# State-space scan moved from VectorE to GpSimd, with low parts moved the other way and masked bias tiles, in a hybrid S5 and attention layer

## The chip, the core and the metric

The kernel runs on one core of a Trainium2 chip. A core has TensorE (PE in the profile; its weight loads are PEld), VectorE (DVE), ScalarE (ACT), GpSimd (POOL) and SyncE (SP), which here issues the transfers. The metric is the device time of one execution, in microseconds, as a median of runs. For the kernel before, that is 2432.99 us (3 runs, 2431.76 to 2434.61).

## The reference, cut to what matters

One layer on x of 2048 tokens by 1024, in float32. Half of the mixing is a diagonal state-space layer, half is chunked attention; then an output projection and a SwiGLU.

```python
proj = rmsnorm(x, norm_mix_g) @ w_in                 # u (512), q, k, v (512 each)
# state-space layer: 32 groups of 16 channels, 64 complex states in each group
states = associative_scan(lam_bar * left + bu)       # bu = b_bar @ u, over 2048 tokens
y_ssm = glu(gelu((c @ states).real + d * u))
# attention: 8 heads of 64; a chunk of 64 frames sees itself and the 8 chunks before
scores = q @ k.T / 8 + bias[h, clip(rel, -128, 128)] # -1e30 outside the band
y_att = softmax(scores) @ v
x = x + concat(rmsnorm(y_ssm), rmsnorm(y_att)) @ w_out
x = x + (silu(h2 @ w_gate) * (h2 @ w_up)) @ w_down   # h2 = rmsnorm(x); then a final rmsnorm
```

## The kernel before, in words

Nearly every product of matrices is made of three matmuls: an operand is split into a high part (a rounded copy, by ACT) and a low part (raw less high, a subtraction by DVE or POOL), and the products high by high, high by low and low by high are summed (`mm3`, `split`, L151).

The phases, with their times in the profiled execution:

1. The input of the state-space layer is projected (`u_phase`, about the first 150 us). Beside it DVE works out the powers of the decay and the tables of the layer (`ssm_prologue`). The tables pass through tensors in HBM.
2. Attention and the state-space layer run interleaved (`att_phase`, about 150 to 830 us). Attention is 128 steps: 4 blocks of 512 tokens, 4 pairs of heads, 2 heads, 4 groups of 128 queries. Of each step come the scores (PE; then DVE adds the bias and takes the minimum, L736; then ACT takes the exponential, L739), two steps later the transposes (PE L77; ACT copies the high part, L754; DVE makes the low part, L755), and after a head's four groups the product with v.
3. Between these, "units" are advanced by a fixed number of yields per step: the projections of q and k (`qk_unit`) and v (`v_unit`) for each block, the normalised input of the block (`hT_unit`: DVE product L638, ACT high part L639, low part L640), and the eight units of the state-space layer (`ssm_unit`), 15 steps each.
4. The mixing, gate, up and down products follow (`mix_phase` and later, to the end).

One unit of the state-space layer takes four groups of 16 channels. It loads its input U and three tables, waits 8 yields, multiplies U with a table, and ACT copies the result into X (L511; 128 partitions, 2 parts, 2 pairs, 256 positions). Then comes the scan on the engine `eng`: seven steps over each eighth position (L525 to L528, four instructions on 128 elements per partition), seven over the ends of the eights in groups (16 elements), three over the groups (4 elements), and the carries back (L536 and L537, 42 and 434 elements). That is 84 instructions. Then four transfers copy the states into XG in another layout (L557), nine yields pass, and PE multiplies U and XG with two tables (`pj<-U,Tm` and `pj<-XG,Vm`).

PE's instructions are kept in the written order (`keep_in_program_order`), so PE stands still at an instruction whose data are late. The other engines and SP take their instructions in an order that the framework's scheduler fixes when the program is built; within an engine the order is then strict, too.

Other places that the change touches: `load_w` (weights of attention are loaded raw, split, and in the first block stored to HBM at L613 for the later blocks, which load them at L615); the bias tile `nb` of each head (loaded at L715 at the head's first step; two memsets on POOL at L716 and L717 put 1e30 into the two corners of 64 by 64 outside the band); and the memset of XG's first column (L554). `k.ssm_eng` and `k.wlo_eng` name the engines of the scan and of the weights' low parts.

Of the kernel before, what the change touches and what calls it, by code (L numbers as in the profile page):

```python
# [13 lines left out]
ALU = mybir.AluOpType  # L14
AX = mybir.AxisListType

P = 128
# [3 lines left out]
NG, CH, NS = 32, 16, 64  # L21
NPR = NG // 2
L = 8
NC = SEQ // L
GB, GP = 4, 2
# [66 lines left out]
def f32(ap):  # L92
    return ap.bitcast(F32)
# [297 lines left out]
def u_phase(k, ident, S):  # L391

    tc, nc, io = k.tc, k.nc, k.io
    with ExitStack() as cx:
        p2 = cx.enter_context(tc.tile_pool(name="u2", side="right", bufs=2))
        p1 = cx.enter_context(tc.tile_pool(name="u1", side="right", bufs=1))
        p3 = cx.enter_context(tc.tile_pool(name="u3", side="right", bufs=4))
        psum = cx.enter_context(tc.tile_pool(name="ups", bufs=6, space=bass.MemoryType.PSUM, reuse_waits="tile"))
        psum2 = cx.enter_context(tc.tile_pool(name="ups2", bufs=2, space=bass.MemoryType.PSUM, reuse_waits="tile"))
        k.pro_psum = psum2  # L400
        wh, wl = k.t(p1, "wuh", [P, KT, DS], F32R), k.t(p1, "wul", [P, KT, DS], F32R)
        rsn = S["rsn"][:].rearrange("p (c j) -> p j c", j=L)
        te = k.te
        X, ST = {}, {}

        def prep(b, each=None):
            acc = k.t(p2, "acc", [P, 512])
            X[b] = []
            for q in range(KT):
                if b == 0:  # L410
                    raw = k.t(p2, "raw", [P, DS])
                    nc.sync.dma_start(raw[:], io["w_u"][q * P : (q + 1) * P, :])
                    nc.scalar.activation(wh[:, q, :], raw[:], AF.Copy, scale=k.gm[:, q : q + 1])
                    nc.vector.scalar_tensor_tensor(wl[:, q, :], raw[:], k.gm[:, q : q + 1], f32(wh[:, q, :]),
                                                   op0=ALU.mult, op1=ALU.subtract)
# [24 lines left out]
        def spread_(b):  # L440
            ps = k.t(psum2, "pp", [P, 512])
            spread(k, te, ps, ST[b], 0)
            nc.scalar.copy(rsn[:, 2 * b : 2 * b + 2, :], ps[:].rearrange("p (j c) -> p j c", j=2))

        def evac(b, f, ps):
            us = k.t(p3, "us", [P, 2, NC], bufs=2)
            nc.vector.tensor_tensor(us[:], ps[:].rearrange("p (j c) -> p j c", j=2), rsn[:, 2 * b : 2 * b + 2, :], op=ALU.mult)
            nc.sync.dma_start(S["u"][f * P : (f + 1) * P, 2 * b : 2 * b + 2, :], us[:])

        def group(b, f):  # L450
            ps = k.t(psum, "ps", [P, 512])
            for q in range(KT):
                mm(b, f, ps, q)
            return ps

        def finish(b, pss):
            with tc.high_priority():
                spread_(b)
                for f in range(4):
                    evac(b, f, pss[f])  # L460

        pss = [k.t(psum, "ps", [P, 512]) for _ in range(4)]

        def first(q):
            for f in range(4):
                mm(0, f, pss[f], q)

        pro = ssm_prologue(k, ident, S)
        prep(0, first)
        next(pro)  # L470
        sums(0)
        held = pss
        for b in range(1, 4):
            prep(b)
            next(pro)
            now = [group(b, 0)]
            finish(b - 1, held)
            now += [group(b, 1), group(b, 2)]
            sums(b)
            held = now + [group(b, 3)]  # L480
        next(pro)
        finish(3, held)
    return pro


def ssm_unit(k, p, psum, S, b, eng):
# [62 lines left out]
    yield from carry(Xe[:, :, :, 1:, :7], Xe[:, :, :, :3, 7], 8, 3)  # L549
    yield from carry(Xk[:, :, :, 1:, :7], Xk[:, :, :, : NC // 8 - 1, 7], 0, NC // 8 - 1)  # L550

    XG = k.t(p, "XG", [P, GB, NC])
    XGv = XG[:].rearrange("p (q g) c -> p q g c", g=2)
    nc.gpsimd.memset(XG[:, :, 0:1], 0.0)  # L554
    for g2 in range(2):
        for c in range(2):
            nc.sync.dma_start(XGv[c * NS : (c + 1) * NS, :, g2, 1:], X[g2 * NS : (g2 + 1) * NS, c, :, : NC - 1])  # L557
    for _ in range(YX):
        yield
    Y = k.t(p, "X", [P, GB, NC])  # L560
# [10 lines left out]
        yield  # L571


SSM_N = YL + GP + 7 + 7 + 3 + 4 + YX + GP


class Unit:
# [21 lines left out]
def att_phase(k, ident, S, pro):  # L599
    tc, nc, io = k.tc, k.nc, k.io  # L600
    with ExitStack() as cx:
        aw = tc.alloc_tile_pool(name="aw", reuse_waits="tile", bufs=1, side="right")
        pfs = cx.enter_context(tc.tile_pool(name="apf", bufs=2, space=bass.MemoryType.PSUM, reuse_waits="tile"))
        hT, vts, qk = {}, {}, {}

        def load_w(sb, n):

            w = k.t(aw, "w", [P, 2, 1024], F32R, bufs=WB)
            if sb == 0:
                raw = k.t(aw, "raw", [P, 1024], bufs=2)  # L610
                nc.sync.dma_start(raw[:], io["w_qk"][n] if n < 8 else io["w_v"][n - 8])
                split(k, w[:, 0], w[:, 1], raw[:], k.wlo_eng)
                nc.sync.dma_start(S["ws"][n], f32(w[:]))  # L613
            else:
                nc.sync.dma_start(f32(w[:]), S["ws"][n])  # L615
            return w[:, 0], w[:, 1]

        def hT_unit(sb, q0=0, q1=KT):
            hi, lo = hT.setdefault(sb, ([], []))
# [12 lines left out]
            for q in range(q0, q1):  # L632
                yield
                load(q + ahead)
                xt = xts[q]
                for v, n in zip(hT[sb], ("hi", "lo")):
                    v.append(k.t(aw, f"{n}{q}x" if q < DB and sb % 2 else f"{n}{q}", [P, SB], F32R))
                nc.vector.scalar_tensor_tensor(xt[:], xt[:], k.gm[:, q : q + 1], S["rsn"][:, ts], op0=ALU.mult, op1=ALU.mult)  # L638
                nc.scalar.copy(hi[q][:], xt[:])  # L639
                (nc.gpsimd if sb or q % 2 else nc.vector).tensor_tensor(lo[q][:], xt[:], f32(hi[q][:]), op=ALU.subtract)  # L640
            yield

        def qk_unit(sb, pr):
# [11 lines left out]
            for c in range(2):  # L655
                ps = k.t(pfs, "pf", [P, 512])
                wh, wl = ws[c]
                for q in range(KT):
                    cs = slice(q * P, (q + 1) * P)
                    mm3(k.ta, ps[:], wh[:, cs], wl[:, cs], hi[q][:], lo[q][:], q == 0, q == KT - 1)  # L660
                    if q < KT - 1:
                        yield
                for hh in range(2):
# [17 lines left out]
        def v_unit(sb, fh):  # L681
# [5 lines left out]
            for i in range(4):  # L687
                ps = k.t(pfs, "pf", [P, 256])
                ic = slice(i * P, (i + 1) * P)
                for q in range(KT):  # L690
# [4 lines left out]
                    k.ta.matmul(ps[:], lo[q][:, ic], wh, start=False, stop=q == KT - 1)  # L695
                    if q % 2 and q < KT - 1:
                        yield
                vt = vts[4 * sb + i, fh]
                pv3 = ps[:].rearrange("p (h d) -> p h d", h=4)
                nc.scalar.copy(vt[:, :, :HD], pv3)  # L700
# [5 lines left out]
        class Head:  # L706
            pass

        def scores(st):
            sb, pr, hh, qp = st  # L710
            h = 2 * pr + hh
            if qp == 0:
                hd = st_head[sb, h] = Head()
                hd.nb = k.t(aa, "nb", [P, 640], bufs=2)
                nc.sync.dma_start(hd.nb[:], bass.AP(S["nb"].tensor, S["nb"].offset + h * 768 + 1, [[1, P], [1, 640]]))  # L715
                nc.gpsimd.memset(hd.nb[0:64, 0:64], 1e30)  # L716
                nc.gpsimd.memset(hd.nb[64:128, 576:640], 1e30)  # L717
                hd.s = {}
                hd.p = None
            hd = st_head[sb, h]  # L720
            q2h, q2l, k2 = qk[sb, pr][hh]
            k0 = max(qp, 4) if sb == 0 else qp
            nk = (qp + 5 - k0) * P
# [762 lines left out]
def block_kernel(tc, io, phases="pusamf"):  # L1486
    nc = tc.nc
    k = K(tc, io)
    k.ssm_eng, k.wlo_eng = nc.vector, nc.gpsimd
    with ExitStack() as cx:  # L1490
        dram = cx.enter_context(tc.tile_pool(name="dram", bufs=1, space=bass.MemoryType.DRAM))
        cp = cx.enter_context(tc.tile_pool(name="const", bufs=1))
# [2 lines left out]
        def pp():  # L1495
# [2 lines left out]
        S = {  # L1498
            "u": k.t(dram, "u", [DS, L, NC]), "y": k.t(dram, "y", [DS, L, NC]),
            "ya": k.t(dram, "ya_s", [NSB, DS, SB]), "x1": k.t(dram, "x1", [D, SEQ]),  # L1500
            "k": k.t(dram, "ks", [2, H, P, SB]), "nb": k.t(dram, "nbs", [H, 768]),
            "bst": k.t(dram, "bsts", [4, P, 8 * P]), "v": k.t(dram, "vs", [NPR, 2, 2, NS, 9 * CH]),
            "hc": k.t(dram, "hc", [2, 7, P, 4, 512]), "h": k.t(dram, "hs", [4, P, HALF]), "ws": k.t(dram, "wss", [12, P, 2, 1024]),
            "hq": k.t(dram, "hq", [2, F2, 7, P, 512]), "wc": k.t(dram, "wc", [F2, 7, P, 512]), "wt": k.t(dram, "wt", [4, P, HALF]),
# [81 lines left out]
```

## Time and profile before

| what | value |
|---|---|
| median of 3 runs | 2432.99 us (2431.76 to 2434.61) |
| profiled execution | 2425.27 us |
| its span, first to last instruction | 2423.5 us |
| mean granted TensorE clock | 0.964 |
| DMA | 425.75 MB |
| 200 to 800 us: PE busy | 523.21 us |
| 200 to 800 us: DVE busy | 456.27 us |
| 200 to 800 us: ACT busy | 300.44 us |
| 200 to 800 us: POOL busy | 58.36 us |

A row of a view by stages gives a stretch of the span, its length, and for each engine the busy time and the number of instructions, then the granted clock, the share of the DMA engines and the rate. A row of a timeline gives start, duration, engine, line, operation, `out<-in` with shapes, and in brackets the idle time of the engine before it and what ended that. A row of waits says who waited for whom: total, times, longest.

### The profile page before, as it was taken

Reading aid. Unit: us, or ns where it says so; the run is one execution under the profiler, and the core shown is the slowest. Engines: PE = TensorE matmul, PEld = TensorE weight load, DVE = VectorE, ACT = ScalarE, POOL = GpSimd, SP = SyncE. Lnnn points to the kernel's source line nnn. Section 1 sums busy time; section 2 is a strip of 40 time slices with the busy share of each in tenths; the row PEclk is TensorE's granted clock in tenths of the full one; section 3 lists DMA queues with packets and bytes.
Section 4 is the critical chain, followed back from the end, with each engine's and each line's share of the span. In section 5 each row is a group of like instructions: output and inputs, shape, how many; then the busy total and the mean of one; then the engine's idle time right before and its main releaser. Section 6 shows DMA issues by size and latency. Waiting matters only on the chain.

```text
span 2423.5 us, 30933 instructions
## 1 busy us (share of the span) xinstructions
PE 2224.6 (92%) x10744; PEld 1862.5 (77%) x10744; DVE 1665.3 (69%) x2943; ACT 1000.3 (41%) x1671; POOL 909.0 (38%) x613
## 2 busy tenths in 40 slices
PE   6876878899998799999999999899999989999996
PEld 5655767788787678877888888688888868888886
DVE  8965688777878675656676666867655456569676
ACT  4233544455544754234333334433333343345322
POOL 4321210010100043257555555755555554445542
PEclk8887999999999999999999999999999989999998
DMA  5655676566554353564455455645433277555551
GB/s 159 174 194 203 216 206 199 174 192 191 169 176 123 121 170 122 183 229 149 135 183 177 158 187 206 237 170 202 154 122 95 71 295 253 190 200 200 182 191 70
DMA packets 223132, 425.75 MB, mean 176 GB/s; under 512 B 30384, under 2 KB 70832, under 8 KB 215872
## 3 DMA queue, kind: packets, MB, share of 16 engines
q1 hardware_dynamic: 222976, 423.79, 53.6%
q8 instruction: 84, 1.38, 0.2%
q14 instruction: 72, 0.59, 0.1%
HBM read 283.97 MB, written 129.26 MB: 171 GB/s over the span
## 4 chain that ended last, share of the span: by engine, by line
PE 56%; DVE 2%; DMA 2%; POOL 1%; issue 1%; ACT 1%; SPq 0%; DVEq 0%; POOLq 0%; ACTq 0%
PE X L74 18%; PE ps L74 18%; PE Y L74 9%; PE big L74 6%; PE W L74 5%; DMA lo<-hc 1%; DVE lo L151 1%; POOL c L151 0%; POOL lo L151 0%; POOL sa L1005 0%; DMA hd<-wc 0%; POOL sa L1004 0%; DVE acc L1451 0%; DVE S L1253 0%; DVE g L1318 0%
## 5 line engine op out<-in xcount | busy, mean ns | idle before, releaser
L74 PE MATMUL X<-hi,c 128*128 128x512 f32 x1408 | 451.2, 391 | 7.9 <-POOL c L151 3.2
L74 PE MATMUL ps<-hd,hd 128*128 128x512 f32 (+1 forms) x1968 | 434.7, 383 | 8.0 <-DVE hd L151 4.6
L74 PEld LDWEIGHTS ps<-hd,hd 128*128 128x128 f32 x1968 | 361.3, 191 | 80.1 <-DVE hd L151 4.9
L151 POOL TENSOR_TENSOR c<-S,c 128x512 fp32r<-128x512 f32 x176 | 251.8, 1432 | 243.8 <-ACT c L150 239.8
L74 PEld LDWEIGHTS X<-hi,c 128*128 128x128 f32 x1408 | 265.1, 188 | 65.5 <-ACT u L1271 4.0
L74 PE MATMUL X<-lo,c 128*128 128x512 f32 x704 | 274.9, 390 | 0.0
L151 POOL TENSOR_TENSOR hd<-hd 128x1536 fp32r<-128x1536 f32 (+1 forms) x53 | 190.3, 3596 | 208.7 <-ACT hd L150 185.5
L150 ACT CAST hd<-hd 128x1536 fp32r<-128x1536 f32 (+1 forms) x106 | 147.4, 1392 | 227.1 <-DMA hd<-hq 155.3
L151 POOL TENSOR_TENSOR c<-raw,c 128x512 fp32r<-128x512 f32 x132 | 189.6, 1436 | 130.6 <-ACT c L150 105.5
L74 PE MATMUL Y<-hi,c 128*128 128x512 f32 x704 | 227.2, 393 | 11.3 <-DVE u L1275 11.3
L1399 DVE TENSOR_TENSOR acc<-acc,ps 128x512 f32<-128x512 f32 x196 | 129.2, 682 | 87.0 <-PE ps L74 84.4
L74 PE MATMUL pf<-hi,w 128*128 128x512 f32 x416 | 157.7, 428 | 10.5 <-ACT hi L639 10.5
L74 PEld LDWEIGHTS Y<-hi,c 128*128 128x128 f32 x704 | 133.5, 190 | 41.0 <-DVE u L1275 13.0
L74 PE MATMUL big<-m,woh 128*128 128x512 f32 x512 | 163.7, 402 | 0.2 <-DVE yr L941 0.2
L150 ACT CAST c<-S 128x512 fp32r<-128x512 f32 x176 | 109.3, 621 | 114.6 <-PE Y L74 57.8
L74 PEld LDWEIGHTS X<-lo,c 128*128 128x128 f32 x704 | 132.7, 188 | 27.3
L716 POOL MEMSET nb<- 64x64 f32 x32 | 4.6, 144 | 387.9 <-DMA nb<-nbs 246.0
L1271 ACT COPY u<-X 128x512 f32<-128x512 f32 x132 | 76.9, 584 | 176.4 <-PE X L74 176.4
L739 ACT ACTIVATE s<-s,mn 128x640 f32<-128x640 f32 (+4 forms) x128 | 97.9, 765 | 121.4 <-DVE mn L736 102.9
L150 ACT CAST c<-raw 128x512 fp32r<-128x512 f32 x132 | 82.1, 622 | 149.7 <-PE Y L74 82.3
L736 DVE CUSTOM_DVE_ANT_0 s<-sc,nb 128x640 f32<-128x640 f32 (+4 forms) x128 | 94.1, 735 | 70.5 <-PE sc L74 56.6
L151 DVE TENSOR_TENSOR hd<-hd 128x1536 fp32r<-128x1536 f32 (+1 forms) x53 | 113.4, 2141 | 35.7 <-ACT hd L150 35.6
(370 smaller groups left out, 4812.2 us busy)
## 6 DMA issues: line engine op xcount, KB each, us to landing
w<-wss SPq DMA_DIRECT2D x36, 1024.0 KB, 5.5
hq<-g SPq DMA_DIRECT2D x140, 256.0 KB, 2.1
hd<-hq SPq DMA_DIRECT2D x42, 768.0 KB, 4.5
hd<-wc SPq DMA_DIRECT2D x42, 768.0 KB, 6.0
raw<-in_w_gate SPq DMA_DIRECT2D x44, 512.0 KB, 3.8
raw<-in_w_up SPq DMA_DIRECT2D x44, 512.0 KB, 4.2
wc<-px SPq DMA_DIRECT2D x66, 256.0 KB, 2.9
wss<-w SPq DMA_DIRECT2D x12, 1024.0 KB, 4.4
```

What stands on the lines that cost most here:

```text
L74: return self.tc.keep_in_program_order(self.tc.nc.tensor.matmul(*a, **b))
L150: nc.scalar.copy(hi, raw)
L151: (lo_eng or nc.gpsimd).tensor_tensor(lo, raw, f32(hi), op=ALU.subtract)
L716: nc.gpsimd.memset(hd.nb[0:64, 0:64], 1e30)
L736: nc.vector.tensor_tensor_reduce(s[:, :nk].rearrange("p (a b) -> p a b", a=nch), ps[:, :nch, :half], hd.nb[:, nk - 1 :: -1].rearrange("p ( ...
L739: nc.scalar.activation(s[:, :nk], s[:, :nk], AF.Exp, bias=mn[:], scale=-1.0, accum_out=sums[sb, pr][:, hh, qp : qp + 1])
L1271: nc.scalar.copy(u[:], ps[:])
L1399: V.tensor_tensor(a, a, ps[:], op=ALU.add)
```

## The change

- `k.ssm_eng` becomes GpSimd: the whole scan runs on POOL. The four transfers of its states (L557) are issued by the same engine, so they move from SP's queue to POOL's.
- XG is one tile for all units; its first column is set to zero once.
- `k.wlo_eng` becomes VectorE: the low parts of the 12 attention weight tiles move from POOL to DVE. So do the low parts of `hT_unit` in all blocks but the first (24 instructions).
- The bias tiles with their corners are written once to a new tensor `nbm` in HBM, in the first phase: one copy from HBM to HBM, and two copies of a constant tile into the corners. A head loads its finished tile, without a memset, and the load is issued two steps before the head begins.
- The stores of split weights (L613) are issued later: in `qk_unit` after the third of eight slices of the product, in `v_unit` after the first of four groups of rows.

```diff
@@ u_phase
+            if b == 2:
+                corner = k.t(p1, "corner", [64, H, 64])
+                nc.gpsimd.memset(corner[:], 1e30)
+                nc.sync.dma_start(S["nbm"][:], bass.AP(S["nb"].tensor, S["nb"].offset + 1, [[768, H], [1, P], [1, 640]]))
+                for m in range(2):
+                    nc.sync.dma_start(S["nbm"][:, m * 64 : m * 64 + 64, m * 576 : m * 576 + 64].rearrange("h p c -> p h c"), corner[:])
@@ ssm_unit
-    XG = k.t(p, "XG", [P, GB, NC])
+    if b == 0:
+        k.XG = k.t(p, "XG", [P, GB, NC])
+        nc.gpsimd.memset(k.XG[:, :, 0:1], 0.0)
+    XG = k.XG
-    nc.gpsimd.memset(XG[:, :, 0:1], 0.0)
...
-            nc.sync.dma_start(XGv[c * NS : (c + 1) * NS, :, g2, 1:], X[g2 * NS : (g2 + 1) * NS, c, :, : NC - 1])
+            eng.dma_start(XGv[c * NS : (c + 1) * NS, :, g2, 1:], X[g2 * NS : (g2 + 1) * NS, c, :, : NC - 1])
@@ att_phase
-                nc.sync.dma_start(S["ws"][n], f32(w[:]))
+                keep[n] = w
...
+        def keep_w(n):
+            if n in keep:
+                nc.sync.dma_start(S["ws"][n], f32(keep.pop(n)[:]))
...
-                (nc.gpsimd if sb or q % 2 else nc.vector).tensor_tensor(lo[q][:], xt[:], f32(hi[q][:]), op=ALU.subtract)
+                (nc.vector if sb or q % 2 == 0 else nc.gpsimd).tensor_tensor(lo[q][:], xt[:], f32(hi[q][:]), op=ALU.subtract)
...
+                    if q == 2:
+                        keep_w(4 * c + pr)
...
+                if i == 0:
+                    for r in range(2):
+                        keep_w(8 + 2 * r + fh)
...
+        def load_nb(h):
+            nb = k.t(aa, "nb", [P, 640], bufs=2)
+            nc.sync.dma_start(nb[:], S["nbm"][h])
+            return nb
...
-                hd.nb = k.t(aa, "nb", [P, 640], bufs=2)
-                nc.sync.dma_start(hd.nb[:], bass.AP(S["nb"].tensor, S["nb"].offset + h * 768 + 1, [[1, P], [1, 640]]))
-                nc.gpsimd.memset(hd.nb[0:64, 0:64], 1e30)
-                nc.gpsimd.memset(hd.nb[64:128, 576:640], 1e30)
+                hd.nb = nbs.pop(h) if nbs else load_nb(h)
...
+            if qp == 2 and (sb, h) < (NSB - 1, H - 1):
+                nbs[(h + 1) % H] = load_nb((h + 1) % H)
@@ block_kernel
-    k.ssm_eng, k.wlo_eng = nc.vector, nc.gpsimd
+    k.ssm_eng, k.wlo_eng = nc.gpsimd, nc.vector
...
-            "k": k.t(dram, "ks", [2, H, P, SB]), "nb": k.t(dram, "nbs", [H, 768]),
+            "k": k.t(dram, "ks", [2, H, P, SB]), "nbm": k.t(dram, "nbms", [H, P, 640]), "nb": k.t(dram, "nbs", [H, 768]),
```

More of the change, by code (lines that the diff above doesn't have):

```diff
@@ L571, in ssm_unit @@
         yield
-SSM_N = YL + GP + 7 + 7 + 3 + 4 + YX + GP
+SSM_N = YL + GP + 7 + 7 + 3 + 4  + YX + GP
 class Unit:
@@ L603, in att_phase @@
         pfs = cx.enter_context(tc.tile_pool(name="apf", bufs=2, space=bass.MemoryType.PSUM, reuse_waits="tile"))
-        hT, vts, qk = {}, {}, {}
+        hT, vts, qk, keep = {}, {}, {}, {}
         def load_w(sb, n):
@@ L707, in att_phase @@
             pass
+        nbs = {}
+        def load_nb(h):
+            nb = k.t(aa, "nb", [P, 640], bufs=2)
+            nc.sync.dma_start(nb[:], S["nbm"][h])
+            return nb
         def scores(st):
```

## The prediction

> **What bounds the kernel now.** I read the page first, then split the stretch in which the state-space layer's eight scans run (217 to 783 us) into the time inside a scan and the time between two scans, then the waits of PE, then single rows. The page says that PE is the busiest engine over the span, so time can be won only where PE stands still:
>
> ```profile
> PE 2224.6 (92%) x10744; PEld 1862.5 (77%) x10744; DVE 1665.3 (69%) x2943; ACT 1000.3 (41%) x1671; POOL 909.0 (38%) x613
> ```
>
> The stages from the first to the last DVE instruction of each scan, and those between, alternate here (columns: length, then busy time and count of PE, PEld, DVE, ACT, POOL, then granted clock and DMA):
>
> ```profile
> 217.60:255.50 37.90, 23.78 (x104) 19.29 (x104) 35.94 (x113) 15.52 (x36) 10.10 (x10) 0.77 0.55 192
> 255.50:297.70 42.20, 36.70 (x216) 32.23 (x217) 20.08 (x54) 21.28 (x58) 10.24 (x10) 0.92 0.72 230
> 297.70:342.50 44.80, 32.46 (x147) 25.45 (x146) 42.39 (x135) 19.17 (x51) 8.18 (x10) 0.92 0.69 209
> 342.50:374.80 32.30, 28.79 (x198) 26.51 (x196) 15.41 (x34) 17.01 (x42) 3.27 (x7) 1.00 0.74 193
> 374.80:417.80 43.00, 37.59 (x210) 31.67 (x208) 41.59 (x124) 20.27 (x39) 0.58 (x4) 1.00 0.64 201
> 417.80:446.50 28.70, 26.17 (x184) 24.73 (x183) 13.21 (x26) 15.48 (x35) 0.40 (x3) 1.00 0.53 129
> 446.50:491.70 45.20, 37.96 (x212) 32.43 (x211) 43.90 (x121) 21.89 (x41) 7.62 (x12) 0.96 0.63 201
> 491.70:524.90 33.20, 32.20 (x218) 29.86 (x217) 18.74 (x34) 19.62 (x41) 4.11 (x6) 1.00 0.73 203
> 524.90:567.00 42.10, 38.04 (x215) 33.22 (x214) 40.70 (x122) 18.99 (x36) 0.87 (x6) 0.96 0.60 192
> 567.00:596.10 29.10, 29.10 (x197) 27.28 (x196) 15.80 (x31) 17.54 (x37) 0.40 (x3) 1.00 0.68 200
> 596.10:638.30 42.20, 35.34 (x206) 30.10 (x206) 40.84 (x119) 19.93 (x38) 5.04 (x9) 0.97 0.53 165
> 638.30:671.40 33.10, 33.10 (x203) 29.99 (x203) 18.89 (x32) 18.95 (x38) 2.70 (x3) 0.98 0.64 171
> 671.40:708.00 36.60, 33.22 (x213) 29.23 (x212) 35.28 (x114) 15.86 (x32) 0.87 (x6) 1.00 0.56 185
> 708.00:744.40 36.40, 33.10 (x194) 29.30 (x193) 19.39 (x34) 20.00 (x40) 0.40 (x3) 1.00 0.56 157
> 744.40:782.50 38.10, 34.64 (x233) 31.63 (x232) 36.81 (x117) 16.72 (x33) 0.87 (x6) 1.00 0.40 120
> ```
>
> Inside a scan DVE is busy 95 to 97% of the time and PE idles 14.1, 12.3, 5.4, 7.2, 4.1, 6.9, 3.4 and 3.5 us, 56.9 in all. Between scans DVE is about half busy and PE idles 5.5, 3.5, 2.5, 1.0, 0, 0 and 3.3 us. So DVE is the limit inside the scans, PE outside, and POOL is nearly free in both. The waits of PE from 200 to 800 us name DVE too:
>
> ```profile
> PE pt L77 <- DVE ptl L755: 30.0, 30, 2.3
> PE sc L74 <- DVE mn L736: 16.4, 8, 10.5
> ```
>
> These two make 46.4 us (total, times, longest). Neither belongs to the scan: they are attention's own evictions, the low parts of the transposes and the minima of the scores, which queue on DVE behind the scan's instructions.
>
> **The scan leaves DVE: the gain.** I give each scan stretch the idle share of PE in the stretch behind it (0.130, 0.109, 0.088, 0.030, 0, 0, 0.091, and the last share again for the eighth). What is left is 4.9, 4.9, 3.8, 1.4, 0, 0, 3.3 and 3.4, together 21.7 us. The granted clock, 0.77 in the first scan and 0.92 in the second against 1.00 later, may rise with it; I count nothing for that. The gain is 56.9 - 21.7 = 35.2 us, by unit 9.2, 7.5, 1.6, 5.9, 4.1, 6.9, 0.1 and 0. At most all 56.9 could go. What is late next is PE itself in units 2 to 7, and in 0 and 1 the small steps of the first block of tokens.
>
> **The scan on POOL: how long.** POOL runs no such small instruction now, so its price comes from larger ones:
>
> ```profile
> 230.40 2.40 POOL L151 TENSOR_TENSOR w<-raw,w 128x1024 fp32r<-128x1024 f32 x1 [9.95 <-ACT w L150]
> 243.88 1.28 POOL L640 TENSOR_TENSOR lo0x<-xt,hi0x 128x512 fp32r<-128x512 f32 x1 [8.35 <-ACT hi0x L639]
> 897.31 1.28 POOL L1004 TENSOR_TENSOR sa<-sa,xt 128x512 f32<-128x512 f32 x1 [4.95 <-issue]
> 898.67 1.28 POOL L1005 TENSOR_TENSOR sa<-sa,xt 128x512 f32<-128x512 f32 x1
> ```
> ```profile
> L527 DVE TENSOR_TENSOR X<-X,st x136: 151/189/512, 218.1 to 770.8; 128x128 f32<-128x128 f32 x56, 128x16 f32<-128x16 f32 x56, 128x4 f32<-128x4 f32 x24
> ```
> ```profile
> L536 DVE TENSOR_TENSOR fx<-X,a x64: 153/596/2691, 239.1 to 781.2; 128x42 f32<-128x42 f32 x32, 128x434 f32<-128x434 f32 x32
> ```
>
> From 512 to 1024 elements POOL pays 1.12 us more: 2.19 ns an element and 0.16 us fixed. The dependent pair at 897 starts 1.36 us apart, 0.08 us over its duration. Four lines like L527 and two like L536, over eight units, give a unit 28 instructions of 128 elements (0.44 us), 28 of 16 (0.195), 12 of 4 (0.17), 8 of 42 (0.25) and 8 of 434 (1.11): 12.3 + 5.5 + 2.0 + 2.0 + 8.9 = 30.7 us, and with 84 gaps of 0.08, 37.4 us. Without the gaps it is 30.7; with half as much again for every one of the 7,888 elements (17.3 us) it is 46.0. I take 37.4, as both rows are of POOL and of the same operation.
>
> Then the four transfers of the states, now queued on POOL behind the scan, in two rows of the tile's view (the first with min, median and max in ns):
>
> ```profile
> L557 SPq DMA_DIRECT2D XG<-X x32: 590/611/1174, 266.0 to 783.2; - x32
> ```
> ```profile
> DMA to landing us min/median/max: 2.3/2.4/5.5
> ```
>
> At SP's price, 4 x 0.61 + 2.4 = 4.8 us; at the dearest, 4 x 1.17 + 5.5 = 10.2. No row has a transfer issued by POOL; I take 4.8. So scan and transfers take 42.2 us. The transfers wait on POOL for the last carry, and behind them stands only the next unit's scan, which needs its own X some 25 us later; SP, where the same waits stood in front of every load, is rid of them.
>
> The Trainium skill ("DMA: Bandwidth & Descriptors", Specifications) gives a first byte about 1 us after issue from GpSimd against 0.6 from Sync; by it 42.2 would be 42.6, and no run here shows it.
>
> **The room that PE leaves.** PE keeps its written order, so it stands still if the states are not there at its first matmul on XG:
>
> ```profile
> L74 PE MATMUL pj<-XG,Vm x64: 378/379/379, 275.1 to 795.2; 128*128 128x256 f32 x64
> ```
> ```profile
> L511 ACT COPY X<-pj x64: 363/367/370, 214.5 to 744.0; 64x256 f32<-64x256 f32 x64
> ```
>
> Eight copies and eight such matmuls belong to a unit. From the start of the scan, which follows the last copy, to the first such matmul there are 57.5 (275.1 - 217.6), 54.0, 52.8, 56.7, 52.3, 56.0, 52.6 and 48.0 us. Less the gains above: 48.3, 46.5, 51.2, 50.8, 48.2, 49.1, 52.5 and 48.0. All are above 42.2.
>
> **POOL and DVE against each other.** While POOL's split of 230.40 ran, a scan instruction of DVE on 16 elements took 2.25 us, where its sister L527, quoted above, has a median of 0.19 over all sizes:
>
> ```profile
> 230.58 2.25 DVE L525 TENSOR_TENSOR st<-X,a 128x16 f32<-128x16 f32 x1
> ```
>
> It ended with POOL's instruction. The Trainium skill ("SBUF — State Buffer", Who interferes with whom) explains it: a DVE instruction with two SBUF inputs and a GpSimd one that reads SBUF exclude each other for a whole instruction. The trace agrees. So each DVE instruction of this kind adds its length to POOL's scan. They are the products of L638, the low parts that move to DVE (24, of the blocks after the first) and the 12 weight splits:
>
> ```profile
> 217.60:262.60 45.00, 0.74 (x1) 0.77 0.60 215
> 297.70:342.70 45.00, 4.56 (x7) 0.92 0.69 209
> 446.50:491.50 45.00, 2.97 (x4) 0.96 0.63 201
> 596.10:641.10 45.00, 2.00 (x3) 0.96 0.56 170
> ```
> ```profile
> 217.60:262.60 45.00, 0.00 (x0) 10.38 (x4) 0.77 0.60 215
> ```
> ```profile
> 869.83 1.22 DVE L151 TENSOR_TENSOR wol<-xt,woh 128x1024 fp32r<-128x1024 f32 x1
> ```
> ```profile
> L640 DVE TENSOR_TENSOR lo<-xt,hi x1: 679/679/679, 169.3 to 169.3; 128x512 fp32r<-128x512 f32 x1
> ```
>
> The first fence counts L638 (DVE) in four scans, the second the splits (POOL). Unit 0 has 0.74 + 4 x 1.22 = 5.6 us, and 42.2 + 5.6 = 47.8 fits in 48.3. Unit 1 has 4.56 + 6 x 0.68 = 8.6: 50.8 against 46.5, a stall of 4.3 us. Unit 3 has 5.7 (47.9 against 50.8), unit 5 has 4.0 (46.2 against 49.1). The stall is 4.3 us in all.
>
> DVE's own added work, 24 x 0.68 + 12 x 1.22 = 31 us, lies in stretches that free over 20 us of DVE per unit: nothing on the path.
>
> **The mask, the stores and the start.** The tiles' two memsets per head go. DVE waited for POOL at these starts of heads:
>
> ```profile
> 273.85 0.29 DVE L736 CUSTOM_DVE_ANT_0 s<-sc,nb 128x128 f32<-128x128 f32 x1 [1.36 <-POOL nb L716]
> ```
> ```profile
> 655.97 0.82 DVE L736 CUSTOM_DVE_ANT_0 s<-sc,nb 128x640 f32<-128x640 f32 x1 [4.00 <-POOL XG L554]
> ```
>
> That is 5.4 us won, since the loads are also issued two steps ahead; if PE had been covered there it is 0. The XG memset becomes one. The stores of split weights leave SP's queue until the split is long done; SP, which queues every other load behind it, gains, and I price it at 0, as no wait of PE above names a weight load. The 12 splits at half POOL's time may win 2 us before 220 us. Against it, the masked tiles are built in HBM in the first phase: 2.6 MB plus corners that must wait on SP for the large copy, with the loads of xt behind them.
>
> ```profile
> DMA packets 223132, 425.75 MB, mean 176 GB/s; under 512 B 30384, under 2 KB 70832, under 8 KB 215872
> ```
>
> At this mean rate it takes 15 us, hidden as long as four tiles are ahead; from 0 to 8 us, I take 2.
>
> **Sum.** -35.2 + 4.3 - 5.4 - 2 + 2 = -36.3 us. The profiled execution took 2425.27 us (span 2423.5), so 2389 there; the median of the runs shown is 2432.99, 7.7 us above it, so 2397.
>
> **Rivals.**
> Scan too long (slower). If a small POOL instruction with several dimensions costs another 0.16 us, as much fixed cost again, a unit takes 42.2 + 13.4 = 55.6 us, and with the exclusion the stalls are 12.9, 17.7, 4.4, 10.5, 7.4, 10.5, 3.1 and 7.6, together 74 us: -35.2 - 5.4 + 74 = +33, 2466 us. It decides from about 51.3 us a unit, 9 us above my sum, or 0.11 us an instruction. For it: the trace has no small two-input instruction of POOL on several dimensions. Against it: the two sizes that the fit rests on leave only 0.16 us fixed, and the gap of 0.08 us is charged 84 times already. Chance 0.21.
>
> Steps over strided elements. The recurrences at L525 to L528 read every eighth float or further apart. If their 4,080 elements a unit cost half as much again, that is 4.5 us: 46.7, stalls 4.0, 8.8, 1.6 and 1.6 in units 0, 1, 3 and 5, and -35.2 - 5.4 + 16 = -24.6, 2408 us. Chance 0.16. The Trainium skill ("GPSIMD Engine Reference", Performance pitfalls for Q7 kernels) states about this surcharge for reads with steps above 8 bytes; no run here shows it.
>
> Nothing won. PE may follow ACT's copies rather than DVE, or the mask's building may cost what DVE yields: -4 to +4 us, 2429 to 2437. Against it: ACT is busy 41 to 48% in the scans and PE's waits name DVE. Chance 0.10.
>
> **How the numbers follow.** Forecast 0.53, with an own range of 2376 (all 56.9 us) to 2414 (10 us of stall more and no mask gain). A measurement here can tell 0.2%, 4.9 us. Faster: 0.53 + 0.16 and a little of the third, 0.71; same 0.07; slower 0.21 and 0.01, 0.22. The range goes from 2374 to 2446: below it little is left, above it about two thirds of the slow rival.
>
> **What the profile after would show.** Right: POOL near 40 us busy per unit, DVE near 55% in the scans, PE idle 3 to 13% there, the first XG matmul not waiting except in unit 1, and 200 to 800 us shorter by about 35. Wrong: PE waiting for XG in every unit (first or second rival), or the first phase longer by over 5 us, or PE still waiting for the softmax evictions with DVE idle.

## The result, and the profile after

The kernel after takes 2406.00 us (median of 4 runs, 2403.77 to 2413.88) beside 2432.38 us for the kernel before (4 runs, 2427.64 to 2434.61): a ratio of 0.990, 95% interval 0.9873 to 0.9927. It is faster by 26 us, where 36 was forecast. The profiled execution has a span of 2401.7 us against 2423.5, 21.8 us less.

The first part of the page of the kernel after shows where work has gone: DVE is 145 us less busy, POOL 228 us more.

```profile
PE 2214.6 (92%) x10744; PEld 1863.5 (78%) x10744; DVE 1520.6 (63%) x2307; ACT 999.0 (42%) x1671; POOL 1137.4 (47%) x1211
```

I cut both spans at three events that both kernels have: the last DVE product of the first phase (L447), ACT's last copy into the first unit's X, and PE's last matmul on XG. Stages of the kernel before (stretch, length, busy times and counts of PE, PEld, DVE, ACT, POOL, granted clock, DMA):

```profile
0.00:147.70 147.70, 112.09 (x480) 89.72 (x480) 132.02 (x360) 46.95 (x78) 44.25 (x36) 0.90 0.55 156
217.50:795.60 578.10, 503.47 (x2988) 442.42 (x2988) 448.77 (x1218) 288.77 (x610) 55.66 (x97) 0.96 0.62 185
795.60:2423.50 1627.90, 1557.80 (x7017) 1290.20 (x7015) 1059.76 (x1327) 634.21 (x916) 788.23 (x468) 0.98 0.50 172
```

The same stages of the kernel after:

```profile
0.00:170.80 170.80, 110.03 (x480) 87.26 (x480) 131.98 (x360) 46.66 (x78) 48.50 (x37) 0.83 0.52 152
240.00:772.90 532.90, 492.72 (x2975) 441.90 (x2974) 303.23 (x571) 286.60 (x606) 292.73 (x704) 0.96 0.67 200
772.90:2401.70 1628.80, 1558.59 (x7017) 1291.91 (x7015) 1055.74 (x1327) 634.84 (x917) 789.87 (x466) 0.98 0.50 172
```

The moderate result is the sum of two large ones. From the first X to the last XG, attention is 45.2 us shorter. The first phase is 23.1 us longer, with nearly the same work on every engine. Between the two nothing changes (69.8 and 69.2 us), and neither does the rest (+0.9).

The eight scans of the kernel after and two of the stretches between them, to be held against the fifteen rows of the prediction:

```profile
240.00:280.70 40.70, 34.21 (x195) 28.93 (x194) 24.39 (x59) 23.98 (x61) 37.24 (x86) 0.96 0.82 286
280.70:304.00 23.30, 19.75 (x122) 17.48 (x122) 12.66 (x28) 12.48 (x33) 1.23 (x3) 1.00 0.66 175
304.00:346.60 42.60, 29.65 (x123) 22.80 (x122) 25.16 (x54) 18.44 (x48) 39.16 (x86) 0.80 0.69 230
346.60:382.30 35.70, 33.07 (x212) 30.34 (x211) 17.07 (x41) 17.45 (x47) 1.21 (x3) 0.95 0.74 199
382.30:419.50 37.20, 37.20 (x218) 33.10 (x217) 22.48 (x39) 21.21 (x40) 33.75 (x86) 1.00 0.76 228
...
446.80:487.00 40.20, 38.05 (x221) 33.82 (x220) 27.38 (x44) 21.94 (x42) 36.78 (x86) 0.96 0.68 224
...
521.40:558.40 37.00, 37.00 (x222) 33.24 (x221) 20.78 (x37) 19.61 (x38) 33.58 (x86) 1.00 0.66 212
...
586.20:624.60 38.40, 36.00 (x218) 32.25 (x218) 25.16 (x41) 20.84 (x41) 34.97 (x86) 0.96 0.61 208
...
655.40:692.50 37.10, 37.10 (x244) 34.19 (x243) 20.82 (x38) 19.70 (x39) 33.68 (x86) 1.00 0.61 200
...
725.10:762.20 37.10, 37.10 (x254) 34.76 (x253) 19.33 (x38) 18.71 (x37) 33.66 (x86) 1.00 0.39 112
```

POOL is now the engine that is nearly full in a scan, DVE is at 52 to 68%, and PE idles 6.5, 13.0, 0, 2.2, 0, 2.4, 0 and 0 us there instead of 56.9 us in all. The waits for the low parts of the transposes and for the minima of the scores, 30.0 and 16.4 us before, have shrunk to these rows of PE's waits from 200 to 800 us:

```profile
PE pt L77 <- DVE ptl L778: 10.1, 8, 2.1
...
PE sc L74 <- DVE mn L759: 1.9, 2, 1.1
```

The loss in the first phase can be read on SP's queue. Its timeline in the kernel before has all eight loads of the second block of x ahead of the first store of the state-space layer's tables:

```profile
24.27 1.85 SPq L417 DMA_DIRECT2D xt<-in_xp  x4
...
30.26 5.90 SPq L417 DMA_DIRECT2D xt<-in_xp  x3
...
44.10 0.35 SPq L417 DMA_DIRECT2D xt<-in_xp  x1
...
47.53 1.40 SPq L343 DMA_DIRECT2D bbs<-bbr  x2
```

The same in the kernel after:

```profile
24.66 1.84 SPq L417 DMA_DIRECT2D xt<-in_xp  x4
26.55 0.78 SPq L479 DMA_DIRECT2D nbms<-nbs  x1
44.66 0.67 SPq L343 DMA_DIRECT2D bbs<-bbr  x1
...
59.77 8.66 SPq L351 DMA_DIRECT2D vs<-v  x8
68.54 2.03 SPq L417 DMA_DIRECT2D xt<-in_xp  x4
```

Four loads of the second block of x are issued at 25 us, then the copy that builds the masked tiles, then twelve stores of the tables, which wait for DVE; only behind them come the other four loads. SP's waits from 20 to 80 us show these stores:

```profile
SPq L343 <- DVE nf L107: 17.8, 1, 17.8
SPq L351 <- DVE v L275: 11.9, 2, 11.6
```

ACT waits for the late loads, and PE for ACT, on their own timelines:

```profile
72.16 0.62 ACT L419 CAST hi<-xt 128x512 fp32r<-128x512 f32 x1 [38.66 <-DMA xt<-in_xp]
```
```profile
72.83 0.79 PE L74 MATMUL ps<-hi,wuh 128*128 128x512 f32 x1 [30.40 <-ACT hi L419]
```

### The profile page after: what moved, and what is told of

Same layout as the page of the kernel before. It is cut to its first block, busy times and chain, and to the rows that moved or that the text cites. A ratio compares the mean times of both kernels' runs of the same rounds, so it can differ in the third digit from the quotient of the medians.

```text
span 2401.7 us, 30858 instructions
## 1 busy us (share of the span) xinstructions
PE 2214.6 (92%) x10744; PEld 1863.5 (78%) x10744; DVE 1520.6 (63%) x2307; ACT 999.0 (42%) x1671; POOL 1137.4 (47%) x1211
## 4 chain that ended last, share of the span: by engine, by line
PE 56%; DVE 3%; DMA 2%; POOL 1%; issue 1%; ACT 1%; SPq 0%; DVEq 0%; ACTq 0%; POOLq 0%
PE X L74 19%; PE ps L74 17%; PE Y L74 9%; PE big L74 6%; PE W L74 5%; DMA lo<-hc 1%; DVE lo L151 1%; DMA hd<-wc 1%; POOL c L151 0%; POOL lo L151 0%; POOL sa L1028 0%; DMA acc<-x 0%; DVE S L1276 0%; POOL sa L1027 0%; DVE g L1341 0%
## 5 line engine op out<-in xcount | busy, mean ns | idle before, releaser
L150 ACT CAST hd<-hd 128x1536 fp32r<-128x1536 f32 (+1 forms) x106 | 147.4, 1392 | 225.3 <-DMA hd<-hq 158.2
L531 POOL TENSOR_TENSOR st<-X,a 128x128 f32<-128x128 f32 (+2 forms) x136 | 46.1, 339 | 260.7 <-ACT X L517 224.8
L74 PE MATMUL Y<-lo,c 128*128 128x512 f32 x352 | 139.0, 395 | 0.0
```

The source lines that it names most:

```text
L74: return self.tc.keep_in_program_order(self.tc.nc.tensor.matmul(*a, **b))
L150: nc.scalar.copy(hi, raw)
L531: eng.tensor_tensor(t[:, :, :, :n], src, ar, op=ALU.mult)
```

## The experiments

The theory at this point: the scan on POOL gives about 45 us in attention, since DVE's evictions no longer queue behind it, and building the masks takes 23 us back by the order of SP's queue. Rivals: the copy's own transfer time; the low parts that moved; and, for the gain, the masks, low parts and late stores rather than the scan. In the table, "first phase" and "attention" are the first two stages as cut above, in the profiled execution of each kernel. Each ratio is to the kernel before as measured beside that run; its median lay between 2426.85 and 2432.38 us.

| kernel | median us | ratio to before (95%) | first phase | attention |
|---|---|---|---|---|
| before (beside the kernel after) | 2432.38 | | 147.7 | 578.1 |
| after | 2406.00 | 0.990 (0.9873 to 0.9927) | 170.8 | 532.9 |
| a_nomask: after, no masked tiles in HBM | 2382.33 | 0.9809 (0.9793 to 0.9825) | 146.9 | 535.2 |
| a_mask0: after, masks stored by the first block | 2391.41 | 0.9831 (0.9807 to 0.9855) | 150.2 | 537.3 |
| a_split: after, the copy in eight parts | 2384.59 | 0.9814 (0.9794 to 0.9834) | 145.8 | 536.5 |
| b_mask: before, masked tiles alone | 2454.20 | 1.0098 (1.0083 to 1.0113) | 170.6 | 583.4 |
| a_dve: after, scan on DVE | 2440.99 | 1.0045 (1.003 to 1.006) | 169.8 | 570.5 |
| b_scan: before, scan alone on POOL | 2488.60 | 1.0246 (1.022 to 1.0273) | 147.7 | 639.9 |
| n_memset_pool: a_nomask, memsets on POOL | 2468.69 | 1.0168 (1.0152 to 1.0183) | 147.4 | 619.4 |
| n_lo_pool: a_nomask, low parts on POOL | 2467.04 | 1.0162 (1.0144 to 1.0179) | 147.8 | 612.6 |
| n_sp_xg: a_nomask, transfers on SP | 2544.77 | 1.0479 (1.0461 to 1.0496) | 147.4 | 696.3 |
| n_extra4: a_nomask, 8 more products a unit | 2385.51 | 0.982 (0.9799 to 0.9841) | 148.3 | 536.4 |
| n_extra8: a_nomask, 16 more products a unit | 2402.86 | 0.9897 (0.9877 to 0.9918) | 147.9 | 554.9 |

**Without the masked tiles (a_nomask).** The build in `u_phase` goes; a head's load is as before, and DVE writes the corners.

```diff
-            if b == 2:
-                corner = k.t(p1, "corner", [64, H, 64])
...
-            nc.sync.dma_start(nb[:], S["nbm"][h])
+            nc.sync.dma_start(nb[:], bass.AP(S["nb"].tensor, S["nb"].offset + h * 768 + 1, [[1, P], [1, 640]]))
+            nc.vector.memset(nb[0:64, 0:64], 1e30)
+            nc.vector.memset(nb[64:128, 576:640], 1e30)
```

> The kernel after, but the masked tiles are not built in HBM: each head loads its bias as in the kernel before and DVE writes the two corners. Theory (the building of the masks alters the order of SP's queue in the first phase, which puts 12 stores of tables in front of the loads of the second block of x, and costs about 22 us there): the last product of the first phase ends near 148 us instead of 171, and the median is 2406 - 22 = 2384 us, give or take 5. Rival (the first phase got longer for another reason, such as the low parts that moved to DVE): the first phase still ends near 171 us and the median stays within 5 us of 2406.

The first phase ends at 146.9 us and the median is 2382.33 us: as the theory had it. The low parts that moved to DVE have no part in the loss. The median is the lowest of the study, 1.9% below the kernel before; a_split, further on, cannot be told from it.

**Masks stored by the first block (a_mask0).** As a_nomask, but a head of the first block also stores its finished tile, and the later blocks load that.

```diff
+            if sb == 0:
+                nc.sync.dma_start(nb[:], bass.AP(S["nb"].tensor, S["nb"].offset + h * 768 + 1, [[1, P], [1, 640]]))
+                nc.vector.memset(nb[0:64, 0:64], 1e30)
+                nc.vector.memset(nb[64:128, 576:640], 1e30)
+                nc.sync.dma_start(S["nbm"][h], nb[:])
+            else:
+                nc.sync.dma_start(nb[:], S["nbm"][h])
```

> The kernel after, but the masked tiles come about in the first block of tokens: each head loads its raw bias, DVE writes the corners, and the tile is stored to HBM for the three later blocks. Nothing of it lies in the first phase. Theory (order of the first phase): 2384 us, within 3 us of the run without stored masks. Rival (the masked tiles save something in the later blocks, where DVE then needs no 48 memsets of about 0.1 us): up to 5 us below that run. If the first phase is slow for another reason: near 2406.

2391.41 us, with runs from 2380.65 to 2393.18. That is above the expectation, and the stored tiles gain nothing: attention takes 537.3 us against 535.2. In the profiled run, 6 us are lost between the first phase and the first X (73.7 against 67.8); what makes them, I did not settle. The same stretch takes 67.6 us in n_extra4 and 72.9 in n_extra8, whose programs are written alike up to there, so it may be a spread between executions.

**The masked tiles alone (b_mask).** The build and the loads of `nbm` in the kernel before, without memsets and without loading ahead.

```diff
+                nc.sync.dma_start(S["nbm"][:], bass.AP(S["nb"].tensor, S["nb"].offset + 1, [[768, H], [1, P], [1, 640]]))
...
-                nc.sync.dma_start(hd.nb[:], bass.AP(S["nb"].tensor, S["nb"].offset + h * 768 + 1, [[1, P], [1, 640]]))
-                nc.gpsimd.memset(hd.nb[0:64, 0:64], 1e30)
-                nc.gpsimd.memset(hd.nb[64:128, 576:640], 1e30)
+                nc.sync.dma_start(hd.nb[:], S["nbm"][h])
```

> The kernel before with the masked tiles alone: built in the first phase as in the kernel after, loaded at each head's first step, no memsets on POOL; the scan stays on DVE. Theory: the first phase ends near 171 us instead of 148, and the waits for memsets (up to 5 us) go, so 2432 + 22 - 3 = 2451 us. Rival (the first phase got longer by the low parts or the scan's move): the first phase ends near 148 us and the time is 2427 to 2433.

2454.20 us, and the first phase ends at 170.6 us. The loss of 23 us belongs to the masks alone; nothing of the expected 3 us shows in attention (583.4 against 578.1), so taking memsets off a POOL that is nearly idle is worth nothing by itself.

**The same copy in eight parts (a_split).** The same bytes at the same place of the program.

```diff
-                nc.sync.dma_start(S["nbm"][:], bass.AP(S["nb"].tensor, S["nb"].offset + 1, [[768, H], [1, P], [1, 640]]))
+                for h_ in range(H):
+                    nc.sync.dma_start(S["nbm"][h_], bass.AP(S["nb"].tensor, S["nb"].offset + h_ * 768 + 1, [[1, P], [1, 640]]))
```

> The kernel after, with the one copy of 2.6 MB that builds the masked tiles cut into eight copies, one for each head; the same bytes at the same place of the program. With that the scheduler leaves SP's queue in nearly the order of before (the loads of the second block of x stand in front of the stores of the tables). Theory (the order of SP's queue is what costs 23 us): the first phase ends at 146 to 155 us, median 2383 to 2393. Rival (the copy's own time on the DMA engines costs it): the first phase ends near 171 us and the median is within 5 us of 2406.

2384.59 us; the first phase ends at 145.8 us. SP's timeline in this kernel has the loads of x in front again:

```profile
24.09 1.84 SPq L417 DMA_DIRECT2D xt<-in_xp  x4
25.97 0.58 SPq L480 DMA_DIRECT2D nbms<-nbs  x1
30.07 3.68 SPq L417 DMA_DIRECT2D xt<-in_xp  x2
33.79 0.48 SPq L480 DMA_DIRECT2D nbms<-nbs  x1
36.73 0.34 SPq L417 DMA_DIRECT2D xt<-in_xp  x1
```

So neither the 2.6 MB nor the wait between copy and corners costs anything. It is the order that the framework's scheduler gave SP's queue in the presence of one large copy. Why it chose that order (it may reckon the copy as long) is argued, not shown.

**Scan back on DVE (a_dve).**

```diff
-    k.ssm_eng, k.wlo_eng = nc.gpsimd, nc.vector
+    k.ssm_eng, k.wlo_eng = nc.vector, nc.vector
...
-            eng.dma_start(XGv[c * NS : (c + 1) * NS, :, g2, 1:], X[g2 * NS : (g2 + 1) * NS, c, :, : NC - 1])
+            nc.sync.dma_start(XGv[c * NS : (c + 1) * NS, :, g2, 1:], X[g2 * NS : (g2 + 1) * NS, c, :, : NC - 1])
```

> The kernel after with the scan back on DVE and its transfers back on SP; masks, low parts on DVE and late stores stay. Theory (all of the gain in attention is DVE's relief by the scan): from the first X to the last product with XG it takes as long as before or longer (575 us, plus up to 10 for the 31 us of low parts on DVE), and with the slow first phase the median is 2450 to 2465 us. Rival (a good part of the gain comes from masks, low parts and late stores): under 2440 us.

2440.99 us, between the two expectations. Attention takes 570.5 us: 37.6 of the 45.2 us hang on the scan and its transfers, and 7.6 us come without them. I had expected that part to be a small loss. PE's waits in this stretch (238 to 809 us) tell the two apart:

```profile
PE pt L77 <- DVE ptl L778: 32.1, 31, 2.4
...
PE sc L74 <- DVE mn L759: 4.0, 7, 1.0
```

With the scan back on DVE, the low parts of the transposes are late again (32.1 us; 30.0 before), so that wait hangs on the scan. The wait for the minima does not: it stays short (4.0 us; 16.4 before). In b_mask, which has neither the memsets nor the loads ahead, it was 16.6 us. In n_lo_pool, with the low parts back on POOL, it is 3.0 us, so the loads ahead or the late stores are the likelier cause; neither was tested by itself.

**The scan alone on POOL (b_scan).**

```diff
-    k.ssm_eng, k.wlo_eng = nc.vector, nc.gpsimd
+    k.ssm_eng, k.wlo_eng = nc.gpsimd, nc.gpsimd
...
-            nc.sync.dma_start(XGv[c * NS : (c + 1) * NS, :, g2, 1:], X[g2 * NS : (g2 + 1) * NS, c, :, : NC - 1])
+            eng.dma_start(XGv[c * NS : (c + 1) * NS, :, g2, 1:], X[g2 * NS : (g2 + 1) * NS, c, :, : NC - 1])
```

> The kernel before with the scan and its transfers on POOL and nothing else: the memsets of the bias tiles, the weights' and the inputs' low parts stay on POOL. Theory (the scan needs POOL to itself, since POOL takes its instructions in order): the scan stands behind memsets that wait for their loads and behind splits, a unit's scan takes 50 to 60 us instead of 37 to 42, PE waits for XG in most units, and the time is 2425 to 2460 us. Rival (DVE's relief is all that counts): the gain of the scan shown by the kernel after against the same with the scan on DVE, 35 us, so about 2395 us.

2488.60 us, 60 us slower than the kernel before beside it (2429.06): slower than either expectation. The scan does not get longer (37.1 to 42.6 us a unit) and PE never waits for XG. The waits are DVE's, from 200 to 870 us:

```profile
DVE s L736 <- POOL nb L717: 49.1, 7, 15.2
DVE s L736 <- POOL nb L716: 41.5, 2, 22.8
```

The two memsets of a head stand behind scan instructions in POOL's order, and the bias of the scores waits for them, up to 22.8 us. So the theory was right that POOL must be free, but wrong about who pays: not the scan, but what stands behind it.

**One part put back at a time on the fastest kernel.** The memsets on POOL (n_memset_pool):

```diff
-            nc.vector.memset(nb[0:64, 0:64], 1e30)
-            nc.vector.memset(nb[64:128, 576:640], 1e30)
+            nc.gpsimd.memset(nb[0:64, 0:64], 1e30)
+            nc.gpsimd.memset(nb[64:128, 576:640], 1e30)
```

> The kernel after without masked tiles (2382 us), but the two memsets of a head's tile on POOL instead of DVE; the load still two steps ahead. Theory (what made the scan alone on POOL slow is that these memsets stand in POOL's order between a scan's instructions and the biases wait for them): DVE's softmax evictions wait for POOL, a few us in most of the heads whose first step falls into a scan, 10 to 60 us slower: 2392 to 2440 us. Rival (in that kernel it was the splits and low parts on POOL): within 4 us of 2382.

2468.69 us, 86 us more than a_nomask, past the end of the expectation. DVE's waits from 200 to 850 us show the same pair of rows as b_scan, even though the loads come two steps ahead:

```profile
DVE s L755 <- POOL nb L725: 51.2, 2, 28.3
DVE s L755 <- POOL nb L726: 51.1, 7, 13.3
```

The low parts of weights and inputs on POOL (n_lo_pool):

```diff
-    k.ssm_eng, k.wlo_eng = nc.gpsimd, nc.vector
+    k.ssm_eng, k.wlo_eng = nc.gpsimd, nc.gpsimd
...
-                (nc.vector if sb or q % 2 == 0 else nc.gpsimd).tensor_tensor(lo[q][:], xt[:], f32(hi[q][:]), op=ALU.subtract)
+                (nc.gpsimd if sb or q % 2 else nc.vector).tensor_tensor(lo[q][:], xt[:], f32(hi[q][:]), op=ALU.subtract)
```

> The kernel after without masked tiles (2382 us), but the low parts of the weights and of the inputs back on POOL. Theory (POOL must be free for the scan): 12 splits of 2.4 us and 24 low parts of 1.3 us stand between scans or behind them, PE waits for low parts in units 0, 1, 3 and 5 or for the states there; 2390 to 2420 us. Rival (POOL has about half of its time free, and DVE gets 31 us back, so it is no loss): 2378 to 2386.

2467.04 us, 85 us more, past the end of the expectation. PE waits for POOL's low parts and for what they hold up (200 to 840 us):

```profile
PE sc L74 <- DVE k L682: 41.7, 3, 23.3
PE pf L74 <- POOL w L151: 29.2, 2, 27.4
PE pf L74 <- POOL lo L646: 15.6, 3, 14.2
```

A split of 2.4 us costs up to 27.4 us when it stands behind most of a scan.

The transfers on SP (n_sp_xg): only the second edit of a_dve.

> The kernel after without masked tiles (2382 us), but the four transfers of the states issued by SP again. Theory (SP takes its instructions in order, so loads stand behind transfers that wait for the scan, as they did before): SP waits some 20 us in all for the scan, and loads of weights and inputs come later; the states land sooner (2.4 us after issue instead of 4.4), which eases units 0, 3 and 7; 2380 to 2392 us. Rival (the queue of the transfers matters in neither way): within 3 us of 2382.

2544.77 us, 162 us more, the largest miss of the study. SP takes the transfers in order and waits for the scan on POOL from 200 to 920 us:

```profile
SPq L559 <- POOL X L537: 195.6, 16, 26.6
```

In the kernel before, SP's transfers of the states waited 23.8 us for the scan on DVE (200 to 800 us); presumably DVE's order had the scan near the place where SP's queue had its transfers. Behind the wait stand the loads of everything else. DVE then waits for biases (`nb`), and PE for DVE:

```profile
DVE nb L725 <- DMA nb<-nbs: 139.4, 16, 24.6
```

I had taken 20 us for the wait of SP from the trace of before without asking how early SP's order places the transfers when the scan is on another engine.

In these three kernels the granted clock over attention is lower too: 0.90, 0.90 and 0.86 against 0.97 in a_nomask. Of the 84.2 us by which attention grows in n_memset_pool, 18.2 are busy time of PE (489.1 to 507.3) and 66.0 are idle time. So each of the three prices holds the waits and what follows from them.

**More work on POOL in front of the transfers (n_extra4, n_extra8).** These kernels do needless work: 8 or 16 products into scratch a unit. They read runs of 32 neighbouring elements, not strided ones as the expectation says.

```diff
+    for _ in range(4):  # 8 in n_extra8
+        pad = k.t(p, "st1", [P, 2, GP, NC // 8])
+        eng.tensor_tensor(pad[:], X[:, :, :, : NC // 8], X[:, :, :, : NC // 8], op=ALU.mult)
+        pad = k.t(p, "st2", [P, 2, GP, NC // 8])
+        eng.tensor_tensor(pad[:], X[:, :, :, : NC // 8], X[:, :, :, : NC // 8], op=ALU.mult)
```

> The kernel after without masked tiles (2382 us), with eight needless products of 128 strided elements on POOL in front of the last two transfers of each unit, 4.2 us by the 0.49 us that the first product of a step takes. Theory (PE stands still when the states land after the room): the states land 0, 6.2, 3.5, 1.6, 3.4, 6.9, 5.8 and 2.4 us ahead of PE, so the stalls grow by 4.2, 0, 0.7, 2.6, 0.8, 0, 0 and 1.8 us, 10 us in all: 2392 us. Rival (the scan is well off the path and no room is short): 2382 us, within 3.

2385.51 us, +3, inside the noise of the rival. The scans grew by about 2.9 us in the units without exclusion (37.2 to 40.1), not 4.2; with 2.9 the same slacks give 2.9 + 1.3 + 0.5 = 4.7 us, which also fits. This run does not tell the two apart.

> As the run with eight needless products, but sixteen of them, 8.4 us a unit. Theory: stalls of 8.4, 2.2, 4.9, 6.8, 5.0, 1.5, 2.6 and 6.0 us, 37 in all: 2419 us, where nearly all that the change of engine gave in attention is gone. Rival (room is not short): 2382 us, within 3.

2402.86 us, +20.5, and attention is 19.7 us longer. That excludes the rival; the 37 us of the theory were too many. The scans grew by 5.8 us (37.2 to 43.0); with that the slacks give 5.8 + 2.3 + 4.2 + 2.4 + 3.4 = 18.1 us. PE's waits from 200 to 780 us now hold 13.6 us at the matmuls on XG, against 3.1 in a_nomask ("issue" there is the same place in units 3, 4 and 7):

```profile
PE pj L74 <- DMA XG<-X: 7.2, 2, 6.3
...
PE pj L74 <- issue: 6.4, 3, 4.1
```

So 10.5 of the 19.7 us are such waits, and 18.1 is near the whole partly by chance: 11.9 us are busy time of PE (489.1 to 500.9), with a granted clock of 0.95 against 0.97. The execution profiled here is also the slowest of its four, 2409.41 us, and that of a_nomask the fastest of its own. The room is real and nearly used up: POOL can take about 3 us more a unit for little, and at 6 us the median rises by 20.

## Why the prediction was right or wrong

**PE's idle time in the scans: right in the sum, in part by luck.** 21.7 us were to be left, 24.0 are; the gain by that is 32.9 against 35.2 us. By unit the errors cancel. Units 2, 6 and 7 were to keep 10.5 us and keep none, and unit 5 was to keep none and keeps 2.4. The largest error is unit 1, where 12.3 became 13.0 instead of 4.9. PE's waits there, from 304 to 347 us, name the input's high parts on ACT (6.7 us), not the scan:

```profile
PE pf L74 <- ACT hi L651: 6.7, 2, 3.6
```

**Why DVE was late: half right.** The prediction laid both waits of PE, 46.4 us, to the scan's instructions on DVE. For the low parts of the transposes that is so; the minima's wait shrank in a_dve with the scan still on DVE.

**Attention as a whole: mis-sized, 45.2 against 36.3 us.** PE's idle time in the whole stretch fell from 74.6 to 40.2 us, 34.4, close to the sum. The other 10.8 us are PE's busy time, 503.47 to 492.72 for nearly the same instructions. The prediction counted nothing for it. The granted clock rose in the first scan (0.77 to 0.96) and fell in the second (0.92 to 0.80), with 0.96 over the stretch both times. It does not explain the difference: the records of these traces hold a granted clock of 1.0 or 0.5 only, and 0.5 stands for 41.0 us of the stretch in both kernels, with PE busy in 31.5 and 33.2 of them. What differs is how often PE stops for more than 0.05 us, 61 times before and 23 after. The two other kernels with the scan on DVE, a_dve and b_mask, stop 63 and 58 times and are busy for 498.6 and 507.4 us. That the stops lengthen the busy time fits this, but no run shows it by itself.

**The scan's length: right, with errors that cancel.** 37.4 us were forecast, 37.0 to 37.2 are measured where nothing disturbs. But the instructions are dearer and the gaps smaller than priced: the durations sum to 34.3 us in such a unit (36.0 in the mean of all eight) against 30.7. Groups of POOL in the kernel after (count, busy, mean in ns), and of the needless products of n_extra8:

```profile
L543 POOL TENSOR_TENSOR X<-X,fx 128x434 f32<-128x434 f32 x32 | 36.5, 1141 | 2.1
L533 POOL TENSOR_TENSOR X<-X,st 128x128 f32<-128x128 f32 x56 | 32.1, 574 | 0.0
L531 POOL TENSOR_TENSOR st<-X,a 128x128 f32<-128x128 f32 x56 | 27.4, 490 | 254.4 <-ACT X L517 224.8 <-DMA Vm<-vs 25.8
...
L565 POOL DMA_DIRECT2D XG<-X x32 | 19.7, 615 | 2.4 <-POOL X L543 2.4
```
```profile
L554 POOL TENSOR_TENSOR st<-X 128x128 f32<-128x128 f32 x64 | 29.2, 457 | 0.6
L556 POOL TENSOR_TENSOR st<-X 128x128 f32<-128x128 f32 x64 | 26.3, 411 | 0.0
```

128 elements cost 0.41 to 0.46 us in runs of neighbours (0.44 was forecast), 0.49 with one strided input and a broadcast factor, 0.57 where input and output are strided. So the strided rival was wrong in its size. The Trainium skill ("GPSIMD Engine Reference", Performance pitfalls for Q7 kernels) gives half as much again per element; these rows have 7 to 40% more per instruction. That the result lies near that rival's 2408 is chance.

**The transfers: underestimated.** 4.8 us from the end of the scan to the last landing were taken; 3.7 to 10.4 are measured, 6.5 in the mean of the units. Two of the four are even issued before the scan ends (in unit 0 at 276.1 and 277.9 us, the scan ends at 280.7), which the sum did not count on. POOL's issue takes 0.615 us, as SP's did, but landing is later than SP's median of 2.4 us (the view of XG):

```profile
DMA to landing us min/median/max: 2.3/4.4/9.4
```

**Room and stall: right in kind, the unit wrong.** The rooms are 44.5, 55.2, 46.0, 52.9, 46.0, 49.9, 47.5 and 44.7 us against 46.5 to 52.5 forecast, the states land 42.1 to 50.7 us after X, and PE waits 3.6 us, in two waits in unit 0, where 4.3 were expected in unit 1:

```profile
PE pj L74 <- DMA XG<-X: 3.6, 2, 1.8
```

Unit 1 kept its idle time and so its room. That the two sizes are close is luck.

**The exclusion of DVE and POOL: about half its price.** Over the 37.1 us of undisturbed units, units 0, 1, 3 and 5 take 3.6, 5.5, 3.1 and 1.3 us more; 5.6, 8.6, 5.7 and 4.0 were added.

**The masks: the step that failed.** "At this mean rate it takes 15 us, hidden as long as four tiles are ahead; from 0 to 8 us, I take 2." It cost 23.1 us. I priced the copy as a transfer and as a wait on SP. a_split has both and loses nothing; what cost was that the other loads changed places with stores that wait for DVE. A first phase longer by over 5 us was among the prediction's own signs of being wrong, and its third rival named the cost ("the mask's building may cost what DVE yields"): half of it was taken back.

**The parts as separate items: too simple.** The prediction gave the memsets with the earlier loads 5.4 us and the low parts 2, or nothing beyond the start. With the scan on DVE that sum is near the truth (7.6 us for all of it, a_dve). With the scan on POOL the memsets, the low parts and the transfers' queue are each worth 85 us or more, as n_memset_pool, n_lo_pool and n_sp_xg show.

**The slow rival.** Its cause occurred only in small part: the instructions came out dearer by 3.6 us a unit, not 13.4, and smaller gaps made up for it. That a longer scan eats the gain is real: 5.8 us more a unit cost 20 us. Its turning point, 9 us more, was not reached by any run.

**The sum.** Attention won 8.9 us more than the 36.3 forecast for it, and the first phase lost 21.1 us more than the 2 forecast. That the total is off by only 10 us in the medians (14.5 between the profiled executions) is in part luck, since the two errors have opposite signs.

## What to carry to other kernels

Before a long chain is moved to an idle engine, list what still stands in that engine's order and who waits for it: a memset of 0.17 us behind a scan of 39.6 us cost DVE 22.8 us at once (b_scan). The queue that issues the chain's transfers belongs to the same list. And one added transfer can cost by the place it gives to others in a queue, so compare the order of the queue before and after, not only the bytes; here cutting the copy into eight gave the 23 us back. Why the scheduler chose the worse order stays open.

## What I had not expected of the hardware

Transfers issued by POOL took a median of 4.4 us from issue to landing, against 2.4 us for the same transfers issued by SP in the kernel before and in n_sp_xg. The issuing engine alone does not make them late: in b_scan, n_memset_pool and n_lo_pool POOL issued them too, and the median was 2.6 us. Those three moved 168 to 174 GB/s in attention; the kernel after and the five others with POOL's transfers moved 194 to 203, with medians of 4.1 to 5.2 us. That other transfers delay them would fit, but no run shows it by itself.

And PE's busy time for nearly the same matmuls differed by 10.8 us of 503 between two kernels whose granted clock was at 0.5 for the same 41.0 us of the stretch.
